# A two-layer trunk on one core: weights of the start in halves, attention norms spread over the head loop, Pool's remainders in pieces

## The chip, the cores and the metric

The kernel runs on one core of a Trainium2 chip. Five engines of that core run side by side, each with its own queue of instructions: TensorE (PE, matrix products), VectorE (DVE), ScalarE (ACT), GpSimd (Pool) and SyncE (SP, which issues nearly all transfers). The metric is the device time of one execution in microseconds (us); lower is better.

## What is computed

`x` is 256 tokens of 1024 numbers, all in fp32. Two layers are run, each a feed-forward part, a token mixer and another feed-forward part; the mixer of layer 0 is a state-space scan (Mamba-2), that of layer 1 an attention with low-rank queries and keys. The change touches the first feed-forward part and the attention:

```python
def rms_norm(x, w):
    return x * rsqrt(mean(x * x, -1) + 1e-6) * w

def swiglu(h, w_gate, w_up, w_down):              # 1024 -> 2816 -> 1024
    return (silu(h @ w_gate) * (h @ w_up)) @ w_down

def mla_mixer(h, positions, ...):                 # 16 heads
    proj = h @ w_in                               # 1024 -> 384 + 256 + 32
    cq = rms_norm(proj[..., :384], q_a_norm)
    ckv = rms_norm(proj[..., 384:640], kv_a_norm)
    k_rope = proj[..., 640:]
    q = (cq @ w_q_b).reshape(b, s, 16, 64 + 32)
    kv = (ckv @ w_kv_b).reshape(b, s, 16, 64 + 64)
    q_nope, q_rope = q[..., :64], q[..., 64:]
    k_nope, v = kv[..., :64], kv[..., 64:]
    # each of q_nope, q_rope, k_nope, k_rope: rms_norm over its own last axis
    # q_rope and k_rope are then turned by the position's angles
    o = causal_block_attention(q_nope, q_rope, k_nope, k_rope, v)   # softmax in blocks of 128 queries
    return o.reshape(b, s, 1024) @ w_out

for i in range(2):
    x = x + 0.5 * swiglu(rms_norm(x), ...)
    x = x + mixer_i(rms_norm(x))
    x = x + 0.5 * swiglu(rms_norm(x), ...)
```

## The kernel before

**Layout.** Features lie on the 128 partitions and the 256 tokens on the free axis, so `x` is eight slices of 128x256. The parts run one after the other: `ffn` 0, `ssm` 1, `ffn` 2, `ffn` 3, `mla` 4, `ffn` 5. The norm's factor for a token is applied after the products: the parts multiply `x` scaled by the norm's weight alone, and the token factors `rs` come in where the products are read.

**Weights.** All weights come as one stream in the order of use, in units of up to eight 128x128 tiles (512 KB). SP's queue loads a unit into one of AHEAD = 4 `raw` buffers. fp32 accuracy is reached by splitting: ACT rounds the unit (L119, `whi`), then `raw - whi` gives the remainder `wlo` (L121) on DVE, or on Pool for the units listed in POOL_UNITS. The rings of `whi` and `wlo` have SPLIT = 5 buffers. A tile is then two or three passes on PE (`mm2` L214, `mm3` L203 to L205, `mm3t` in `mla`). Two units of the attention (EARLY) are loaded and split during `ffn(3)`, in buffers of their own.

**Start.** SP issues `nw`, then slices of `x` and units of weights in turn, then the constants `sm` and `cst`. The first two units hold four tiles. Each slice of `x` is scaled and split (`xp`: ACT L232, DVE L233) and squared and summed on Pool (L239 to L243). After the first 32 tiles of `ffn(0)`, `make_rs` sums the squares on PE (L249), takes mean and epsilon on DVE (`rsv`, L253) and the power -1/2 on Pool (`rsc`, L257), and spreads the result on PE (L264); only then can the four open accumulators be read by the gated products (L320, L321) and given back.

**Attention.** `latent` writes cq and ckv in two parts. DVE turns the 32 rotary features of the keys into `kr`. `half(i)` then does eight heads: two groups of four heads of queries (`qc`), keys (`kc`), values (`vt`), with sums of squares by DVE reductions (L863, L879), then `rsqrt` by eleven dependent DVE instructions (L807 to L821), then the scaling of `qc` on DVE and of `kc` on Pool (L896), then `rope` with two products on Pool, two on DVE (L833) and two sums on DVE (L838, L841). `half(0)` and `half(1)` both run before the head loop. The loop over heads `h` turns heads h+2, h+3 (`to_heads`, L909, transposes on PE), makes the scores of head h (L947 to L952, with two mask products, `idb` times `neg`; then `mx` and `pr` on DVE and ACT, L957 to L966), turns the weights of head h-2 (`turned`, L974, and the copy `pT`), multiplies the values of head h-4 (L987, L988), and from h = 12 on does one step of the output projection. In `values` two heads share one accumulator, one on each half of the array's columns.

**Order.** The Tile scheduler places the instructions of each engine from the program's order and its own estimates; each engine then works through its list in that order, and waits where an input is missing.

Of the kernel before, what the change touches and what calls it, by code (L numbers as in the profile page):

```python
# [10 lines left out]
F32 = mybir.dt.float32  # L11
# [36 lines left out]
def unit_sizes():  # L48
# [13 lines left out]


POOL_UNITS = [MLA0 + n for n in (15, *range(17, 26))]
EARLY = (MLA0 + 10, MLA0 + 16)


class Stream:
# [11 lines left out]

    def load(self, upto):
        while self.loaded < min(upto, len(self.sizes)):
            u = self.loaded
            if u in EARLY:
# [4 lines left out]
            self.nc.sync.dma_start(  # L89
                t[:, : n * P],  # L90
                self.src[self.offs[u] : self.offs[u + 1]].rearrange("(p c) -> p c", p=P),
            )
            self.raw[u] = t
            self.loaded += 1

    def cut(self, upto):
        while self.split < min(upto, len(self.sizes)):
# [8 lines left out]
            if self.sizes[u] == KD * NARROW // P:  # L106
# [12 lines left out]
            self.nc.scalar.copy(hi[:, :n], raw[:, :n])  # L119
            eng = self.nc.gpsimd if u in POOL_UNITS else self.nc.vector  # L120
            eng.tensor_tensor(  # L121
                out=lo[:, :n], in0=raw[:, :n], in1=hi[:, :n].bitcast(F32), op=ALU.subtract
            )
            self.parts[u] = (hi, lo)

    def early(self, pool, u):
# [6 lines left out]
        hi = pool.tile([P, n], F32R, name=f"hi{u}", bufs=1)  # L133
        lo = pool.tile([P, n], F32R, name=f"lo{u}", bufs=1)
# [6 lines left out]
    def ahead(self):  # L141
        self.load(self.unit + SPLIT)
        self.cut(self.unit + SPLIT - 1)
# [21 lines left out]
def trunk(ctx: ExitStack, tc: tile.TileContext, xt, pos, wts, small, consts, out):  # L165
# [19 lines left out]
    nc.sync.dma_start(nw, small[:, S_NW : S_NW + KD])  # L185
    ws = Stream(nc, wp, wts)
    for i, (d0, d1) in enumerate(((0, 1), (1, 2), (2, 4), (4, 6), (6, 8))):
        nc.sync.dma_start(x[:, d0:d1], xt[:, d0:d1])
        ws.load(i + 1)
    nc.sync.dma_start(sm, small)  # L190
    nc.sync.dma_start(cst, consts)
# [93 lines left out]
    def use_x(n, d):  # L285
# [5 lines left out]
        scaled_parts(xh[:, d], xl[:, d], x[:, d], w)  # L291
        if d == 0:
            accs[n] = sp.tile([P, T], F32, tag="xsq", name="xsq")
# [18 lines left out]
    def ffn(n, nxt, early=()):  # L312
        early = list(early)
        with tc.tile_pool(name="fp", bufs=2) as fp:
# [20 lines left out]
            for k in range(KD):  # L335
                for o in ps:
                    mm2(o, ws.next(), xp[:, k], k == 0, k == KD - 1)
            rs, rh = make_rs(n, True)
            for j in range(2):
                gated(j, ps[2 * j], ps[2 * j + 1])  # L340
            for q in range(2, KF):
# [5 lines left out]
                if early and q % 2 == 0:  # L347
# [389 lines left out]
    def mla(n, nxt):  # L737
        with tc.tile_pool(name="lp", bufs=2) as lp:
# [14 lines left out]
            neg = one("neg", [P, P], BF16)  # L753
            nc.vector.tensor_copy(idb, ident)
            nc.vector.tensor_copy(neg, cst[:, C_NEG : C_NEG + P])

            oh = one("oh", [P, 8, T], F32R)
            ol = one("ol", [P, 8, T], F32R)
# [23 lines left out]
            p0, p1 = acc_ps(), acc_ps()  # L782
            for k in range(KD):
                a = (xh[:, k], xl[:, k], k == 0, k == KD - 1)
                mm3(p0[:, :T], ws.next(), *a)
# [412 lines left out]
```

## Time and profile before

| | |
|---|---|
| median of three runs | 1120.55 us (1119.16 to 1121.17) |
| the profiled execution | 1121.53 us, of which the span of the trace is 1119.4 us |
| PE busy | 1083.5 us (97%) |
| DVE busy | 846.4 us (76%) |
| ACT busy | 642.2 us (57%) |
| Pool busy | 216.9 us (19%) |
| mean granted clock of PE | 0.989 |
| transfers | 191.58 MB, mean 171 GB/s |

"Busy" is the union of an engine's instructions, so an engine at 97% can still be the one that waits in the remaining 3%. The granted clock is the share of full speed at which PE was allowed to run: 1.00 is the upper of its two levels (2.4 GHz), 0.50 the lower (1.2 GHz).

### The profile page before, as it was taken

The numbers are of one execution on the slowest core, as the hardware profiler recorded it, in microseconds if no ns is written. First come the engines' busy times: TensorE is split into PE (matmuls) and PEld (weight loads), VectorE is DVE, ScalarE is ACT, GpSimd is POOL, SyncE is SP. The second block draws the span as 40 slices with busy tenths as digits, with TensorE's granted clock in tenths as the row PEclk, the third lists the DMA queues.
The fourth block names the chain that finished last, engine by engine and source line by source line (L and its number), as shares of the span: only waits on it lengthen the run. The fifth ranks groups of instructions, "written<-read, shape, count | busy, mean of one in ns | idle before, by whom it ended". The sixth has DMA issues, their size and how long they took to land.

```text
span 1119.4 us, 18325 instructions
## 1 busy us (share of the span) xinstructions
PE 1083.5 (97%) x6902; PEld 967.1 (86%) x6902; DVE 846.4 (76%) x1370; ACT 642.2 (57%) x1102; POOL 216.9 (19%) x201
## 2 busy tenths in 40 slices
PE   7999999998899998999999999999996999999998
PEld 6888888998899997888888888888995788888887
DVE  7877776789978767877776787767779768877663
ACT  6766544667775744655544565554565546655541
POOL 7000012203523236000012200002347035000000
PEclk9999999999999999999999999999998999999999
DMA  7766565555445444655555565555443025665661
GB/s 243 229 188 190 192 187 172 177 191 191 160 148 186 137 149 133 202 187 186 186 184 180 192 226 188 188 188 181 162 145 103 1 66 171 214 189 185 189 202 55
DMA packets 55320, 191.58 MB, mean 171 GB/s; under 512 B 6304, under 2 KB 8384, under 8 KB 55232
## 3 DMA queue, kind: packets, MB, share of 16 engines
q1 hardware_dynamic: 55200, 190.41, 52.2%
q8 instruction: 54, 0.88, 0.3%
q14 instruction: 34, 0.28, 0.1%
q0 software_dynamic: 32, 0.00, 0.0%
HBM read 189.31 MB, written 1.08 MB: 170 GB/s over the span
## 4 chain that ended last, share of the span: by engine, by line
PE 57%; DVE 4%; POOL 1%; ACT 1%; issue 0%; ACTq 0%; DVEq 0%
PE acc L214 31%; PE misc L214 16%; PE acc L203 2%; PE acc L204 2%; PE acc L205 2%; PE acc L987 1%; POOL xsq L243 1%; DVE qc L896 1%; POOL sq L242 1%; PE misc L949 1%; PE misc L909 1%; PE misc L974 0%; PE misc L947 0%; PE acc L988 0%; DVE ro L833 0%; ACT whi L119 0%
## 5 line engine op out<-in xcount | busy, mean ns | idle before, releaser
L121 DVE TENSOR_TENSOR wlo<-raw,whi 128x1024 fp32r<-128x1024 f32 (+3 forms) x345 | 433.6, 1259 | 153.6 <-ACT whi L119 152.5
L119 ACT CAST whi<-raw 128x1024 fp32r<-128x1024 f32 (+3 forms) x355 | 364.8, 1032 | 258.0 <-PE acc L214 137.5
L214 PE MATMUL misc<-xp,whi 128*128 128x512 f32 x704 | 278.0, 398 | 1.4 <-ACT whi L119 1.4
L214 PE MATMUL acc<-xp,whi 128*128 128x512 f32 x704 | 274.4, 393 | 0.0
L214 PE MATMUL acc<-ap,whi 128*128 128x512 f32 x616 | 215.5, 397 | 0.0
L214 PE MATMUL misc<-xp,wlo 128*128 128x256 f32 x704 | 196.5, 281 | 2.6 <-DVE wlo L121 2.5
L214 PE MATMUL acc<-xp,wlo 128*128 128x256 f32 x704 | 197.1, 282 | 0.5 <-DVE wlo L121 0.3
L214 PE MATMUL acc<-ap,wlo 128*128 128x256 f32 x616 | 167.7, 281 | 0.0
L214 PEld LDWEIGHTS acc<-xp,whi 128*128 128x128 f32 x704 | 131.9, 188 | 32.0
L214 PEld LDWEIGHTS misc<-xp,whi 128*128 128x128 f32 x704 | 132.0, 188 | 23.9 <-ACT whi L119 1.6
L214 PEld LDWEIGHTS misc<-xp,wlo 128*128 128x128 f32 x704 | 132.4, 188 | 11.0 <-DVE wlo L121 4.0
L214 PEld LDWEIGHTS acc<-ap,whi 128*128 128x128 f32 x616 | 113.9, 188 | 25.6
L214 PEld LDWEIGHTS acc<-xp,wlo 128*128 128x128 f32 x704 | 132.5, 188 | 1.8 <-DVE wlo L121 1.1
L214 PEld LDWEIGHTS acc<-ap,wlo 128*128 128x128 f32 x616 | 115.4, 188 | 2.8
L320 ACT COPY g<-misc 128x256 f32<-128x256 f32 x88 | 32.7, 371 | 79.6 <-PE misc L214 79.4
L204 PE MATMUL acc<-xp,whi 128*128 128x256 f32 x264 | 74.6, 283 | 0.0
L203 PE MATMUL acc<-xp,whi 128*128 128x256 f32 x264 | 74.4, 283 | 0.0
L239 POOL TENSOR_TENSOR xsq<-x 128x256 f32<-128x256 f32 x6 | 3.7, 614 | 364.6 <-DVE x L364 350.1
L205 PE MATMUL acc<-xp,wlo 128*128 128x256 f32 x264 | 74.2, 281 | 0.0
L242 POOL TENSOR_TENSOR sq<-x 128x256 f32<-128x256 f32 x42 | 40.3, 967 | 114.5 <-DVE x L364 112.1
L243 POOL TENSOR_TENSOR xsq<-xsq,sq 128x256 f32<-128x256 f32 x45 | 51.7, 1149 | 2.6
L321 DVE TENSOR_TENSOR g<-misc,g 128x256 f32<-128x256 f32 x88 | 37.1, 422 | 18.2 <-ACT g L320 18.2
(249 smaller groups left out, 1908.3 us busy)
## 6 DMA issues: line engine op xcount, KB each, us to landing
raw<-wts SPq DMA_DIRECT2D x341, 512.0 KB, 3.9
acb<-acd SPq DMA_DIRECT2D x8, 512.0 KB, 4.1
raw<-wts SPq DMA_DIRECT2D x8, 256.0 KB, 2.8
raw<-wts SPq DMA_DIRECT2D x4, 384.0 KB, 3.0
out<-x SPq DMA_DIRECT2D x8, 128.0 KB, 3.4
x<-xt SPq DMA_DIRECT2D x3, 256.0 KB, 6.3
raw<-wts SPq DMA_DIRECT2D x4, 192.0 KB, 2.3
sm<-small SPq DMA_DIRECT2D x1, 283.5 KB, 6.6
```

Source lines behind the costliest of these rows:

```text
L119: self.nc.scalar.copy(hi[:, :n], raw[:, :n])
L121: eng.tensor_tensor(out=lo[:, :n], in0=raw[:, :n], in1=hi[:, :n].bitcast(F32), op=ALU.subtract)
L203: nc.tensor.matmul(o, w[0], h, start=start, stop=False)
L204: nc.tensor.matmul(o, w[0], l, start=False, stop=False)
L205: nc.tensor.matmul(o, w[1], h, start=False, stop=stop)
L214: nc.tensor.matmul(dst, a, b, start=start and i == 0, stop=stop and i == 1)
L242: nc.gpsimd.tensor_tensor(out=sq, in0=src, in1=src, op=ALU.mult)
L243: nc.gpsimd.tensor_tensor(out=acc, in0=acc, in1=sq, op=ALU.add)
L320: nc.scalar.copy(t, ps[:, T:])
L321: nc.vector.tensor_tensor(out=t, in0=ps[:, :T], in1=t, op=ALU.add)
L896: eng.tensor_tensor(out=a, in0=a, in1=r[:, b, o].unsqueeze(2).broadcast_to(list(a.shape)), op=ALU.mult,)
L909: nc.tensor.transpose(ps[:QK, o : o + P], src[:, b, h0 + h], ident)
```

## The change

1. **Start.** The first four units all hold eight tiles, and are loaded, rounded and subtracted in halves of 512 columns; each half's load follows the load of one slice of `x`. `nw` is loaded by Pool's queue. `cst` and `sm` are loaded after the first 32 tiles' code. The squares of the first norm are made by two ACT instructions of 1024 columns and three DVE sums; Pool takes no part in them.
2. **EARLY** holds four units (all those of keys and values) in place of two.
3. **Attention norms.** Keys' and values' latents come first. The norms of the heads are three: `a` (keys of heads 0 to 7, queries of 0 to 3), `b` (queries 4 to 7), `c` (keys and queries 8 to 15). `a` and `b` run before the loop; the four steps of `c` are put into the head loop at h = 1 to 4, each behind the scores of head h-2. Pool does none of the scalings and rotary products; ACT copies the rotary keys into `kc`.
4. **Head loop.** Both masks are one product of 256 columns; the values of two heads are multiplied together at odd h.
5. **Pool.** POOL_UNITS are eight units of the output projection; each remainder is four pieces of 256 columns, and waits for the last scaling made so far by a norm.

```diff
-    ffn = [4] * 2 + cut(KF * KD * 2 - 8) + cut(KD * KF)
+    ffn = cut(KF * KD * 2) + cut(KD * KF)
-    mla = cut(KD * 5) + narrow + ([6, 3] * 2 + [8] * 2) * 2 + cut(64)
+    mla = cut(KD * 5) + narrow + ([8] + [6, 3] * 2 + [8]) * 2 + cut(64)
...
-POOL_UNITS = [MLA0 + n for n in (15, *range(17, 26))]
-EARLY = (MLA0 + 10, MLA0 + 16)
+HALVED = KD // 2
+POOL_UNITS = [MLA0 + n for n in range(18, 26)]
+EARLY = (MLA0 + 6, MLA0 + 11, MLA0 + 12, MLA0 + 17)
...
+            for c in self.pieces(u):
+                if u < HALVED:
+                    next(self.beside)
+                self.nc.sync.dma_start(t[:, c], src[:, c])
...
+            for c in self.pieces(u):
+                self.nc.scalar.copy(hi[:, c], raw[:, c])
+            for c in self.pieces(u, 4 if u in POOL_UNITS else 1):
+                ins = eng.tensor_tensor(
+                    out=lo[:, c], in0=raw[:, c], in1=hi[:, c].bitcast(F32), op=ALU.subtract
+                )
+                if u in POOL_UNITS and self.behind is not None:
+                    self.tc.add_manual_dep(
+                        ins.ins, self.behind.ins.name,
...
-    nc.sync.dma_start(nw, small[:, S_NW : S_NW + KD])
+    nc.gpsimd.dma_start(nw, small[:, S_NW : S_NW + KD])
...
+            if n == 0:
+                nc.sync.dma_start(cst, consts)
+                nc.sync.dma_start(sm, small)
+                sq = fp.tile([P, KD, T], F32, name="x2", bufs=1)
+                for h in (slice(0, 4), slice(4, 8)):
+                    nc.scalar.activation(sq[:, h], x[:, h], AF.Square)
+                for h in (4, 2, 1):
+                    nc.vector.tensor_tensor(
+                        out=sq[:, :h], in0=sq[:, :h], in1=sq[:, h : 2 * h], op=ALU.add
+                    )
+                accs[n] = sq[:, 0]
...
-            half(0)
-            half(1)
+            for b in range(NB):
+                nc.scalar.copy(kc[:, b, :, NOPE:], krt[:, b].broadcast_to([P, MH, ROPE]))
+            keys(0, ss[0])
+            queries(0, ss[0], 8, 4)
+            for _ in normed("a", ss[0], (0, 8), (0, 4)):
+                pass
+            queries(1, ss[1], 0, 4)
+            for _ in normed("b", ss[1], (4, 4), (4, 8)):
+                pass
+            values_of(0)
+            ws.limit = MLA0 + 18
+            steps = normed("c", ss[2], (8, 16), (8, 16))
+            def second(h):
+                if h == 0:
+                    keys(1, ss[2])
+                    queries(2, ss[2], 8, 8)
+                    queries(3, ss[2], 12, 8)
+                    values_of(1)
+                if 0 < h < 5:
+                    step = next(steps)
...
+                if h == 5:
+                    ws.limit = len(SIZES)
+                    ws.cut(MLA0 + 21)
...
-                if 0 <= h - 4 < MH:
-                    values(h - 4, pTs.pop(h - 4))
+                if 0 <= h - 4 < MH and h % 2:
+                    values((h - 5) // 2, [pTs.pop(h - 5), pTs.pop(h - 4)])
+                second(h)
```

ACT's first instructions, before (`whi` of 512 columns is a unit of four tiles):

```order
L183 COPY used<-ones 128x1
L232 ACTIVATE xp<-x,nw 128x256
L119 CAST whi<-raw 128x512
L232 ACTIVATE xp<-x,nw 128x256
L119 CAST whi<-raw 128x512
L232 ACTIVATE xp<-x,nw 128x256 x2
L119 CAST whi<-raw 128x1024
```

ACT's first instructions, after (`x_249` is the tile of squares):

```order
L204 COPY used<-ones 128x1
L131 CAST whi<-raw 128x512
L256 ACTIVATE xp<-x,nw 128x256 x2
L131 CAST whi<-raw 128x512
L256 ACTIVATE xp<-x,nw 128x256
L131 CAST whi<-raw 128x512
L256 ACTIVATE xp<-x,nw 128x256
L370 ACTIVATE x_249<-x 128x1024
L131 CAST whi<-raw 128x512
L256 ACTIVATE xp<-x,nw 128x256
```

The first rounding of weights moved ahead of the first slice of `x`, every rounding became one of 512 columns, and the squares entered ACT's list.

DVE at the end of the second half's sums of squares, before (all of it ahead of the first scores):

```order
L863 TENSOR_REDUCE ss_9200<-qsq 128x4 x3
L879 TENSOR_REDUCE ss_9200<-ksq 128x8
L863 TENSOR_REDUCE ss_9200<-qsq 128x4 x2
L889 TENSOR_SCALAR ss_9200<-ss_9200 128x2x8
L879 TENSOR_REDUCE ss_9200<-ksq 128x8
L838 TENSOR_TENSOR qc<-ro 128x2x8x16
L841 TENSOR_TENSOR qc<-ro 128x2x8x16
```

DVE in the first heads of the loop, after (`nyc` is the result of norm `c`'s `rsqrt`):

```order
L1050 TENSOR_SCALAR pr<-pr,sums 128x128
L1050 TENSOR_SCALAR pr<-pr,sums 128x256
L930 TENSOR_TENSOR kc<-kc,nyc 128x2x8x64
L1041 TENSOR_REDUCE mx<-misc 128x1
L1048 RECIPROCAL sums<-sums 128x2
L1061 COPY pT<-misc 128x384
L1041 TENSOR_REDUCE mx<-misc 128x1
L1050 TENSOR_SCALAR pr<-pr,sums 128x128
L1050 TENSOR_SCALAR pr<-pr,sums 128x256
L930 TENSOR_TENSOR qc<-qc,nyc 128x2x8x32
```

The scalings of the second half now stand between the scores of the first heads, not ahead of them.

PE in the head loop, before (`pT`, `vt` are the values' operands; L909 turns heads):

```order
L974 MATMUL misc<-cst,pr 128x128 x3
L909 MATMUL misc<-cst,kc 96x128 x4
L987 MATMUL acc<-pT,vt 64x256
L988 MATMUL acc<-pT,vt 64x128
L909 MATMUL misc<-cst,qc 96x128 x4
L947 MATMUL misc<-kT,qT 128x128
```

PE in the head loop, after:

```order
L1057 MATMUL misc<-cst,pr 128x128 x3
L963 MATMUL misc<-cst,kc 96x128 x4
L1072 MATMUL acc<-pT,vt 64x256
L963 MATMUL misc<-cst,qc 96x128 x4
L1072 MATMUL acc<-pT,vt 64x256
L1072 MATMUL acc<-pT,vt 64x128 x2
L1032 MATMUL misc<-kT,qT 128x256
```

The values of two heads moved together, with a turn of queries between the first product of 256 columns and the second, while the two of 128 columns stand side by side.

## Rows read from the trace of the kernel before

**Rows 1.** Waits of PE, 823 to 874 us: engine, line, releaser: total, times, longest.

```profile
PE misc L909 <- DVE qc L841: 9.7, 1, 9.7
```

**Rows 2.** Stretches: PE, PEld, DVE, ACT, POOL busy (count), PEclk, DMA share, GB/s.

```profile
823.98:873.69 49.71, 37.54 (x202) 32.05 (x201) 44.68 (x112) 32.67 (x63) 28.40 (x20) 0.90 0.37 113
826.00:845.00 19.00, 19.00 (x101) 17.53 (x101) 17.21 (x53) 16.09 (x28) 9.41 (x8) 1.00 0.52 158
845.00:860.00 15.00, 4.92 (x22) 3.29 (x22) 14.90 (x20) 7.71 (x12) 14.35 (x8) 0.81 0.40 129
873.00:895.00 22.00, 21.82 (x148) 16.38 (x147) 14.78 (x51) 11.91 (x42) 0.00 (x0) 1.00 0.00 1
```

**Rows 3.** Stretches around PE's long wait, same columns.

```profile
854.26:859.68 5.42, 0.00 (x0) 0.00 (x1) 5.42 (x5) 2.77 (x5) 5.08 (x3) 0.50 0.61 174
859.68:864.50 4.82, 4.82 (x21) 4.22 (x22) 2.49 (x13) 1.91 (x4) 2.04 (x2) 0.50 0.23 77
```

**Rows 4.** Stretches of the start, same columns.

```profile
6.43:27.02 20.59, 16.59 (x85) 12.77 (x86) 19.68 (x31) 14.03 (x23) 18.14 (x23) 1.00 0.77 272
9.00:11.00 2.00, 1.51 (x8) 1.06 (x8) 1.52 (x3) 1.65 (x3) 1.92 (x4) 1.00 1.04 417
```

**Rows 5.** PE at the start, order of time: start, us, instruction [idle before <-releaser].

```profile
6.43 0.50 PE L214 MATMUL misc<-xp,whi 128*128 128x512 f32 x1 [1.42 <-ACT whi L119]
...
21.48 0.50 PE L249 MATMUL misc<-ones,xsq 128*128 128x1 f32 x4
...
27.02 0.43 PE L264 MATMUL misc<-cst,rsc 128*128 128x128 f32 x2 [0.87 <-POOL rsc L257]
```

**Rows 6.** ACT, DVE and Pool at the start, same columns, one engine after another.

```profile
5.76 0.62 ACT L119 CAST whi<-raw 128x512 fp32r<-128x512 f32 x1 [1.52 <-DMA raw<-wts]
...
4.28 0.48 DVE L233 SCALAR_TENSOR_TENSOR xp<-x,nw,xp 128x256 fp32r<-128x256 f32 x1
...
8.11 0.68 DVE L121 TENSOR_TENSOR wlo<-raw,whi 128x512 fp32r<-128x512 f32 x1
...
25.33 1.64 POOL L257 TENSOR_TENSOR rsc<-rsv,mhalf 128x2 f32<-128x2 f32 x1 [0.23 <-DVE rsv L253]
```

**Rows 7.** Pool, then DVE, in the first norm of the heads, same columns.

```profile
837.80 5.24 POOL L121 TENSOR_TENSOR wlo<-raw,whi 128x1024 fp32r<-128x1024 f32 x2 [0.40 <-ACT whi L119]
...
838.34 2.41 DVE L821 SCALAR_TENSOR_TENSOR nyh<-nth,nyh 128x48 f32<-128x48 f32 x1
...
843.14 0.21 DVE L818 SCALAR_TENSOR_TENSOR nth<-nth,nvh 128x48 f32<-128x48 f32 x1
843.39 0.21 DVE L821 SCALAR_TENSOR_TENSOR nyh<-nth,nyh 128x48 f32<-128x48 f32 x1
```

**Rows 8.** DVE's groups, 824 to 873.69 us: instruction | busy, mean ns | idle before.

```profile
L879 DVE TENSOR_REDUCE ss<-ksq 128x8 f32<-128x512 f32 x4 | 2.7, 675 | 0.0
...
L121 DVE TENSOR_TENSOR wlo<-raw,whi 128x768 fp32r<-128x768 f32 x2 | 1.9, 958 | 0.0
```

**Rows 9.** DVE in the attention, order of time, columns as in rows 5.

```profile
823.98 0.41 DVE L799 TENSOR_TENSOR kr<-acc,rs 64x256 f32<-64x256 f32 x1
...
828.68 0.60 DVE L863 TENSOR_REDUCE ss<-qsq 128x4 f32<-128x256 f32 x2
...
871.59 0.41 DVE L838 TENSOR_TENSOR qc<-ro 128x256 f32<-128x256 f32 x1
```

**Rows 10.** PE in the head loop, and one row of the scan (`ssm`), same columns.

```profile
873.69 0.49 PE L974 MATMUL misc<-cst,pr 128*128 128x128 f32 x3
...
874.94 0.65 PE L987 MATMUL acc<-pT,vt 128*64 128x256 f32 x2
...
290.96 0.66 PE L571 MATMUL misc<-dec,xd 128*64 128x256 f32 x4
```

**Rows 11.** Pool and DVE late in the head loop, same columns.

```profile
908.24 2.38 POOL L121 TENSOR_TENSOR wlo<-raw,whi 128x1024 fp32r<-128x1024 f32 x1 [8.04 <-ACT whi L119]
...
908.86 2.10 DVE L966 TENSOR_SCALAR pr<-pr,sums 128x128 f32<-128x128 f32 x2
```

More of the change, by code (lines that the diff above doesn't have):

```diff
@@ L79, in __init__ @@
         self.unit, self.pos = 0, 0
+        self.tc, self.behind = None, None
+        self.limit = len(SIZES)
     def load(self, upto):
@@ L118, in cut @@
             lo = self.pool.tile([P, UNIT * P], F32R, tag="wlo", name="wlo", bufs=SPLIT)
-            self.nc.scalar.copy(hi[:, :n], raw[:, :n])
             eng = self.nc.gpsimd if u in POOL_UNITS else self.nc.vector
-            eng.tensor_tensor(
-                out=lo[:, :n], in0=raw[:, :n], in1=hi[:, :n].bitcast(F32), op=ALU.subtract
-            )
+            for c in self.pieces(u):
[7 more added lines that the diff above has]
+                        ins.ins, self.behind.ins.name,
+                        mybir.DependencyInfo(
+                            mybir.DependencyClass.Sync, mybir.DependencyReason.DATA
+                        ),
+                        reason="the port that DVE and Pool share",
+                    )
             self.parts[u] = (hi, lo)
@@ L184, in trunk, with load_x @@
     nw = cp.tile([P, KD], F32, name="nw")
-    nc.sync.dma_start(nw, small[:, S_NW : S_NW + KD])
+    nc.gpsimd.dma_start(nw, small[:, S_NW : S_NW + KD])
+    def load_x():
+        for d in range(KD):
+            yield nc.sync.dma_start(x[:, d], xt[:, d])
     ws = Stream(nc, wp, wts)
[L187 to L191, printed above, removed]
+    ws.tc = tc
+    ws.beside = load_x()
+    ws.load(HALVED)
     ident = cst[:, C_ID : C_ID + P]
@@ L346, in ffn @@
                 gated(q, pg, pu)
-                if early and q % 2 == 0:
+                if early and q % 4 == 0:
                     ws.early(*early.pop(0))
@@ new lines, in normed, with scaled @@
+            def normed(name, ss, hk, hq):
+                (k0, k1), (q0, q1) = hk, hq
+                nk, nq = k1 - k0, q1 - q0
+                ro = ss[:, :, nk + nq :]
+                first = nc.vector.tensor_scalar_mul(ro, ro, NOPE / ROPE)
+                r = rsqrt(ss.rearrange("p b s -> p (b s)"), NOPE, name)
+                r = r.rearrange("p (b s) -> p b s", b=NB)
+                yield first
+                def scaled(s0, a):
+                    return nc.vector.tensor_tensor(
+                        out=a, in0=a,
+                        in1=r[:, :, s0 : s0 + a.shape[2]].unsqueeze(3)
+                        .broadcast_to(list(a.shape)),
+                        op=ALU.mult,
+                    )
+                if nk:
+                    yield scaled(0, kc[:, :, k0:k1, :NOPE])
+                a = qc[:, :, q0:q1, NOPE:]
+                first = scaled(nk + nq, a)
+                rope(a, a, nq, qtab)
+                yield first
+                ws.behind = scaled(nk, qc[:, :, q0:q1, :NOPE])
+                yield ws.behind
@@ L880, in half, with values_of @@
+            def values_of(i):
                 w = [ws.next(4), ws.next(4)]
@@ L955, in scores @@
                 pr = lp.tile([P, 3 * P], F32, tag="pr", name="pr", bufs=4)
-                for b, sl in ((0, slice(0, P)), (1, slice(P, 3 * P))):
+                for b, sl in ((0, slice(T, 3 * P)), (1, slice(0, T))):
                     nc.vector.tensor_reduce(
```

197 lines of the change are left out of this document (99 added, 98 removed).

## The prediction

> **What bounds the kernel now.** I read the busy shares first: TensorE is busy nearly throughout, so only a place where it stands idle, or runs at its lower clock, can give time back. Its list of waits names one large place: 9.7 us in the attention, where the first turn of heads waits for DVE's last rotary sum (`qc`, L841) [rows 1]. The stretches around it show the pattern [rows 2]: from 826 to 845 PE is busy for all of its 19 us, from 845 to 860 for 4.9 of 15, while DVE is busy for 14.9 and Pool for 14.35 of those 15; from 873 on PE is full again. After the wait PE works at half its clock: 4.82 us of work at a granted clock of 0.50, the lower of its two levels, which is 2.4 us lost, after 5.42 us in which it ran nothing [rows 3]. The second place is the start: between its first weight product (6.43) and the spread of the first norm (27.02) PE works 16.59 of 20.59 us, and the last wait there is on Pool's power [rows 4, 5]. The feed-forward parts elsewhere are PE's own work, and the change leaves their products as they are; the two further units fetched early in `ffn(3)` add a load, an ACT rounding and a Pool remainder each, to a stage where PE waits for none of these engines, so I cost them at nothing (bounds: 0 to one remainder on Pool, 2.4 us [rows 11], if PE ever waited for one).
>
> **The sum's base** is the profiled execution, 1121.53 us. It lies 1.0 above the median of the runs, which I take off at the end.
>
> **Part 1, the start.** What goes: the whole-unit steps of load, rounding and remainder, and Pool's chain of squares. What comes: a rounding of 512 columns at 0.62 and a remainder at 0.68 per half [rows 6].
> - First product: its weights land at 5.76 before [rows 6]; one issue less stands ahead of them on SP (`nw` moved to Pool's queue; the two units' start-to-start issues are some 0.45 apart, an estimate), so 5.3. The rounding (0.62), the remainder of weights (0.68) and the low part of `x` (0.48) follow; in the new order the first rounding is ahead of the first slices of `x`, so 5.3 + 0.62 + 0.68 + 0.48 = 7.1, against 6.43: 0.67 later. `nw` from Pool's queue can be late by as much without cost, since ACT first waits for the weights.
> - From there PE's work to the spread of the norm is the same 16.59 us [rows 4]. If it never waited, the spread would come at 7.1 + 16.6 = 23.7 instead of 27.02: -3.3. That is one bound. What could eat it up is the supply of halves. PE makes eight products of a half, at 16.59 us for 85 some 0.195 each [rows 4], so 1.5 us per half. A half and its slice of `x` are 384 KB, 0.94 us at the 417 GB/s of 9 to 11 us, where the transfers are full (DMA share 1.04 [rows 4]); DVE needs 0.68 + 0.48 = 1.16 us per half [rows 6], ACT about as much and the squarings besides. So each of the three keeps ahead of PE, but ACT with little to spare. The other bound is 0, if PE waits behind the squarings as long as it now waits for whole units.
> - The norm itself: two squarings of 1024 columns on ACT and sums of 1024, 512 and 256 on DVE are done well before the 32nd tile's column sums; then sums, `rsv` and the same power on Pool (1.64 [rows 6]) run beside PE's next group, as before, without the squares ahead of them. `cst` and `sm`, issued behind two more units, are first read at the spread; they displace no weights any more.
> I take -2.8, inside 0 to -3.3, nearer to PE's own pace, since all three suppliers are faster than PE.
>
> **Part 2, the norms of the heads.** Removed: Pool's share (two rotary products, the keys' scaling), the wait of DVE behind Pool, and the second half's norm from ahead of the loop. Before, from `kr` at 823.98 [rows 9] to the turn of head 2's weights at 873.69 [rows 10] pass 49.7 us; PE works 37.5 of them, 2.4 of which are lost to the clock [rows 2, 3]. The same work of PE has to be done by the same point after, so PE alone would allow 35.1 us: -14.6. I think DVE comes later than that. Its list up to that point, at undisturbed prices:
> - remainders of four query units, 2 x 0.96 and 2 x 0.55 (the smaller by columns) [rows 8]: 3.0
> - sums of squares, 4 x 0.68 [rows 8] and 8 pairs x 0.60 [rows 9]: 7.5
> - four `rsqrt` chains of 11 dependent instructions, 0.21 each and 0.23 to 0.25 from start to start [rows 7]: 10.3
> - the rotary key's preparation, a dozen instructions of about 0.21 [rows 7]: 2.6
> - scalings: two of 1024 columns, the rest 256 or 512 columns, at 0.41 per 256 [rows 9] falling to 1.2 per 1024 by the remainders' rate [rows 8]: 5.0
> - rotary products and sums, two sets of six at some 0.22 and one set of six at 0.35 to 0.41 [rows 9]: 4.7
> - scores of three heads and the maximum of the fourth: DVE is busy 14.78 us for 51 instructions in the loop, 6.5 per head, so 1.9 us per head [rows 2]: 6.4
> The sum is 39.5 us, so the third turn at 863.5 instead of 873.69: **-10.2**. The prices of before can't be taken, since there DVE stood behind Pool: one instruction of 48 columns took 2.41 us beside Pool's remainder, its like 0.21 a little later [rows 7]. Bounds: -14.6 if PE sets the end; -6 if the chain is a tenth longer and a half-clock spell stays.
>
> **Part 3, the rest of the loop and Pool's pieces.** The loop before is PE's: 21.82 of 22 us [rows 2], about 2.8 us a head against DVE's 1.9.
> - Values: in the scan four products on the two column halves take 0.66 us together; in the loop two take 0.65 [rows 10]. So two heads' products can overlap. In the new order only those of 128 columns stand together; between those of 256 a turn of queries stands. A pair of 128 columns is a third of a pair's values, an estimated 0.2 us saved for each of eight pairs: -1.6 (bounds: 0; all overlapped, 8 x 0.8 = -6.4, by 0.65 and a half of it for the shorter ones, less what they already share).
> - Masks: one product in place of two, -0.4. At the third turn one more head's values are already done: -0.8.
> - Norm `c` leaves a rotary set and two scalings, some 3.4 us on DVE, for heads 3 and 4; DVE then needs more than PE per head: +1.0.
> - Pool's pieces: beside a remainder of 1024 columns that took 2.38 us, two instructions of 128 columns on DVE took 2.10 us, where 256 columns alone take 0.41 [rows 9, 11]. A quarter of it lasts 0.6. DVE has 0.9 us a head to spare. Of 32 pieces, 12 come close together behind h = 5; bounds 0 to +3.6 (12 x 0.6 over four heads, less 4 x 0.9). I take +0.7, since most pieces meet a DVE that has room.
> Sum: -1.1. The Trainium skill (SBUF — State Buffer, "SBUF: two separate sides") says that DVE and GpSimd share one port pair as an exclusive lock, held for a whole instruction, the loser blocked. Row 908.86 agrees; by that rule every piece could hold up DVE for its length, and this term would be the bound +3.6 instead of +0.7.
>
> **Sum:** 1121.5 - 2.8 - 10.2 - 1.1 = 1107.4; less 1.0 for the median: **1106.4**.
>
> **Rivals.**
> - *PE sets the end of the norms* (start -3.3, norms -14.6, loop -1.1, median -1.0): 1101.5; with all values overlapping too, 4.8 lower, 1096.7. For it: 35.1 us of PE work in that stretch. Against it: DVE's list is longer than that, and hardly anything on it can go. The Trainium skill (TensorEngine Tiling (Array Packing), "Key Properties") says that different tiles of the array execute in parallel; the scan's row agrees, but the order of the loop parts the longer products.
> - *The gains are halved:* the start gains nothing (0), DVE's chain ends at -6, pieces cost +3.6 (loop +1.8): 1121.5 - 6 + 1.8 - 1.0 = 1116.3. For it: DVE in this stretch is dependent small instructions, with ACT's exponentials between; against it: the scheduler interleaves two chains.
> - *Slower, by the clock:* with the one long wait replaced by many short ones between 830 and 873, PE may run at its lower level. 35.1 us of work at half the clock are 70; it decides from the point where PE works over 15 us of them at half: 35.1 + 15 is as long as before, and with all of it the end is 20 later, 1138. For it: the row at 0.50 after a wait [rows 3]. Against it: with PE busy, though in pieces, the clock held 1.00 from 826 to 845 [rows 2].
> - *It doesn't do what it says:* norm `b`, still ahead of the loop, keeps the first turn of heads waiting as before; DVE's list up to there is some 12 us shorter, so I hold it unlikely. Time: 1120.
>
> **Chances:** forecast (1103 to 1110) 0.62, PE-bound 0.12, halved gains 0.16, slower 0.06, no effect 0.04. The range 1100 to 1114 leaves out the lower part of the second, the upper part of the third and the last two. About 0.2% is what a measurement can tell from no change; faster by more than that 0.90, within it 0.04, slower 0.06.
>
> **What would show it.** The wait of the first turn of heads should shrink from 9.7 us to under 4, and the stretch at 0.50 with it; DVE should be busy without a break from `kr` to the third turn, some 39 us; the spread of the first norm should come at about 24 us. In the loop DVE's instructions beside Pool's pieces should be longer by 0.6 us at most. I am wrong if `rsqrt` instructions still take over a microsecond each, if PE's waits only move to scores and `pT`, or if the granted clock stays at 0.50 in the loop.

## The result and the profile after

The changed kernel takes 1104.37 us (median of four runs, 1102.76 to 1106.05), the kernel before 1120.74 on the same chip: a ratio of 0.9857, 95% interval 0.9839 to 0.9874, so 16 us faster, where 14 were forecast. The profiled execution is one of 1104.49 us with a span of 1102.7, against 1121.53 and 1119.4: 17 us. Its busy shares, engine by engine:

```profile
PE 1079.8 (98%) x6886; PEld 964.3 (87%) x6886; DVE 838.8 (76%) x1396; ACT 643.1 (58%) x1105; POOL 195.7 (18%) x201
```

Five marks cut both executions into the same stretches. They are, in order of time in the trace of the changed kernel, the spread of the first norm, the first column sum of the scan (`ssm`), `kr`, the turn of head 2's weights, and the first column sum of the last feed-forward part (start, us, instruction; between the brackets the idle time before it and what ended it):

```profile
23.09 0.43 PE L288 MATMUL misc<-cst,rsc 128*128 128x128 f32 x2 [1.14 <-POOL rsc L281]
...
200.26 0.28 PE L273 MATMUL misc<-ones,xsq 128*128 128x1 f32 x2
...
819.32 0.42 DVE L837 TENSOR_TENSOR kr<-acc,rs 64x256 f32<-64x256 f32 x1
...
856.85 0.52 PE L1057 MATMUL misc<-cst,pr 128*128 128x128 f32 x3 [0.88 <-ACT pr L1044]
...
923.04 0.50 PE L273 MATMUL misc<-ones,xsq 128*128 128x1 f32 x4
```

In the kernel before the first, third and fourth are in [rows 5, 9, 10], and the other two are:

```profile
202.64 0.28 PE L249 MATMUL misc<-ones,xsq 128*128 128x1 f32 x2
...
940.10 0.50 PE L249 MATMUL misc<-ones,xsq 128*128 128x1 f32 x4
```

(The profile puts the four column sums of a mark in one row or in two; the start of the first counts.) Out of these:

| stretch | before | after | difference | forecast |
|---|---|---|---|---|
| to the spread of the first norm | 27.02 | 23.09 | -3.9 | -2.8 |
| to the scan | 175.6 | 177.2 | +1.6 | 0 |
| scan, two feed-forward parts, latents, to `kr` | 621.3 | 619.1 | -2.3 | 0 |
| `kr` to the third turn | 49.7 | 37.5 | -12.2 | -10.2 |
| third turn to the end of the attention | 66.4 | 66.2 | -0.2 | -1.1 |
| last feed-forward part | 179.3 | 179.7 | +0.4 | 0 |

The largest change is where it was looked for. The stretches of the changed kernel, to be held against [rows 2] (busy time of PE, PEld, DVE, ACT, Pool, then the granted clock): from `kr` to the third turn as a whole, 19 us within it, and the stretch in which Pool runs 20 of its pieces.

```profile
819.32:856.85 37.53, 34.72 (x197) 30.04 (x196) 32.69 (x133) 30.77 (x65) 1.77 (x3) 1.00 0.20 63
826.00:845.00 19.00, 19.00 (x106) 17.36 (x105) 17.82 (x82) 18.58 (x34) 0.00 (x0) 1.00 0.27 85
858.53:872.47 13.94, 12.68 (x72) 8.84 (x72) 11.68 (x30) 8.89 (x27) 13.94 (x20) 0.88 0.46 145
```

PE works 34.7 of 37.5 us at full clock, where it worked 37.5 of 49.7. Pool, busy for 28.4 us of that stretch before, is busy for 1.8. In place of one wait of 9.7 us PE has these from `kr` on, of which 2.8 us lie ahead of the third turn and 1.6 behind it (engine, line, releaser: total, times, longest):

```profile
PE misc L1057 <- ACT pr L1044: 1.2, 2, 0.9
PE misc L963 <- DVE pT L1061: 1.0, 1, 1.0
PE misc L1057 <- DVE sums L1048: 0.6, 1, 0.6
PE misc L1032 <- ACT kT L968: 0.6, 1, 0.6
PE misc L963 <- ACT pr L1044: 0.5, 1, 0.5
PE acc L1072 <- DVE pT L1061: 0.5, 1, 0.5
```

### The profile page after: what moved, and what is told of

It is laid out like the page before. It is cut to its first block, busy times and chain, and to the rows that moved or that the text cites. A ratio compares the mean times of both kernels' runs of the same rounds, so it can differ in the third digit from the quotient of the medians.

```text
span 1102.7 us, 18308 instructions
## 1 busy us (share of the span) xinstructions
PE 1079.8 (98%) x6886; PEld 964.3 (87%) x6886; DVE 838.8 (76%) x1396; ACT 643.1 (58%) x1105; POOL 195.7 (18%) x201
## 4 chain that ended last, share of the span: by engine, by line
PE 61%; DVE 2%; ACT 0%; issue 0%; ACTq 0%; DVEq 0%
PE acc L238 32%; PE misc L238 17%; PE acc L227 2%; PE acc L228 2%; PE acc L229 2%; PE acc L1072 1%; PE acc L248 1%; PE acc L247 1%; PE acc L249 1%; PE misc L963 1%; PE misc L1032 1%; PE misc L1057 0%; DVE pr L1050 0%; DVE mx L1041 0%; PE misc L1033 0%; PE misc L273 0%
## 5 line engine op out<-in xcount | busy, mean ns | idle before, releaser
L134 DVE TENSOR_TENSOR wlo<-raw,whi 128x1024 fp32r<-128x1024 f32 (+2 forms) x345 | 429.4, 1247 | 155.0 <-ACT whi L131 153.8
L131 ACT CAST whi<-raw 128x1024 fp32r<-128x1024 f32 (+2 forms) x353 | 362.8, 1032 | 252.5 <-PE acc L238 132.9
L238 PEld LDWEIGHTS acc<-xp,whi 128*128 128x128 f32 x704 | 131.9, 188 | 32.2
L346 ACT COPY g<-misc 128x256 f32<-128x256 f32 x88 | 32.7, 371 | 77.1 <-PE misc L238 77.1
L266 POOL TENSOR_TENSOR sq<-x 128x256 f32<-128x256 f32 x35 | 31.7, 912 | 111.2 <-DVE x L402 111.2
L227 PEld LDWEIGHTS acc<-xp,whi 128*128 128x128 f32 x264 | 49.7, 189 | 0.3 <-issue 0.3
```

The costliest lines, as they stand in the source:

```text
L131: self.nc.scalar.copy(hi[:, c], raw[:, c])
L134: ins = eng.tensor_tensor(out=lo[:, c], in0=raw[:, c], in1=hi[:, c].bitcast(F32), op=ALU.subtract)
L227: nc.tensor.matmul(o, w[0], h, start=start, stop=False)
L238: nc.tensor.matmul(dst, a, b, start=start and i == 0, stop=stop and i == 1)
L266: nc.gpsimd.tensor_tensor(out=sq, in0=src, in1=src, op=ALU.mult)
L346: nc.scalar.copy(t, ps[:, T:])
```

## The experiments

Each kernel is the changed one with one thing altered, unless it says otherwise, and each was compared with the kernel before on the same chip. "kr to third" and "third to end" are the stretches of the table above, from each profile.

| kernel | median us | ratio to before (95%) | kr to third | third to end |
|---|---|---|---|---|
| before | 1120.74 | 1 | 49.7 | 66.4 |
| changed | 1104.37 | 0.9857 (0.9839 to 0.9874) | 37.5 | 66.2 |
| old_start | 1108.69 | 0.9897 (0.9884 to 0.9911) | 37.6 | 66.2 |
| start_only (on before) | 1117.08 | 0.9972 (0.9959 to 0.9985) | 50.6 | 66.4 |
| c_ahead | 1107.47 | 0.9884 (0.9870 to 0.9897) | 41.7 | 64.4 |
| pool_norms | 1104.91 | 0.9863 (0.9849 to 0.9876) | 39.3 | 65.6 |
| pool_whole | 1107.59 | 0.9869 (0.9852 to 0.9885) | 37.5 | 68.7 |
| whole_free | 1110.32 | 0.9895 (0.9875 to 0.9915) | 46.7 | 63.3 |
| no_pool_units | 1108.12 | 0.9873 (0.9856 to 0.9890) | 37.6 | 68.6 |
| early_two | 1105.09 | 0.9853 (0.9830 to 0.9877) | 39.1 | 65.5 |
| all_three | 1114.44 | 0.9943 (0.9927 to 0.9960) | 50.9 | 62.4 |
| warm_spread | 1105.06 | 0.9864 (0.9849 to 0.9880) | 37.6 | 64.5 |
| later_steps | 1103.16 | 0.9841 (0.9828 to 0.9854) | 36.0 | 67.1 |
| best | 1103.64 | 0.9854 (0.9827 to 0.9880) | 36.0 | 66.6 |

Medians of different rows come from different chips (before: 1120.0 to 1122.1), so the ratios are to be compared. An interval is some 1.5 to 3 us wide either way; single stretches of a profile tell smaller things apart: `kr` to the third turn is 37.5 or 37.6 us in the changed kernel and in the four that don't alter it there (`old_start`, `pool_whole`, `no_pool_units`, `warm_spread`). Not always, though: `start_only` has the code of before there and 50.6 us instead of 49.7, with 3.4 us more at the lower clock.

### The start, undone and alone

`old_start` has the start of before in the changed kernel, `start_only` the new start in the kernel before:

```diff
-HALVED = KD // 2
+HALVED = 0
-    ffn = cut(KF * KD * 2) + cut(KD * KF)
+    ffn = [4] * 2 + cut(KF * KD * 2 - 8) + cut(KD * KF)
...
+    for i, (d0, d1) in enumerate(((0, 1), (1, 2), (2, 4), (4, 6), (6, 8))):
+        nc.sync.dma_start(x[:, d0:d1], xt[:, d0:d1])
+        ws.load(i + 1)
```

> The changed kernel with the start of before (two units of four tiles, whole units, squares on Pool, nw on SP). The trace of the changed kernel gained 3.93 us up to the spread of the first norm, but only 2.38 us of it are left at the end of the first feed-forward part, where its products come every 0.1761 us instead of 0.1737. Theory: that slower pace belongs to the new start, so undoing the start costs only 2.4 us, and the pace is 0.174 again: 1106.8 us, with 1.5 us either way for half-clock spells in the scan. Rival: the pace has nothing to do with the start; undoing it costs 3.9 us, 1108.3, and the pace stays 0.176.

> The kernel before with the new start alone (four units in halves beside the slices of x, squares on ACT and DVE, nw on Pool's queue). Theory that the parts add up: spread of the first norm near 23.1 instead of 27.0, pace 0.176 in the first feed-forward part, so 2.4 us faster than before, 1118.3. Rival that the start's gain reaches the end whole: 1116.8. Rival that a later stage gives it back: 1120.5.

Undoing the start costs 0.40% (0.9897 against 0.9857), 4.5 us; alone it brings 0.28%, 3.1 us. The totals lie nearer to the rivals, but their intervals also take in the 2.4 us of the theories; it is the pace that decides. The slower pace in the first feed-forward part, which hid 1.6 us of the gain in the profile of the changed kernel, is no part of the start: `start_only` and `c_ahead` have the new start and the quicker pace. (In `old_start`, where the rival expected the slower one, it is quick too.) Counted over the same 90 us (50 to 140, PE busy throughout), the kernel before, the changed kernel and `c_ahead`, in that order:

```profile
50.00:140.00 90.00, 90.00 (x520) 79.02 (x519) 68.17 (x113) 54.34 (x98) 0.00 (x0) 1.00 0.61 190
...
50.00:140.00 90.00, 90.00 (x513) 78.38 (x512) 66.75 (x110) 52.94 (x95) 0.00 (x0) 1.00 0.61 187
...
50.00:140.00 90.00, 90.00 (x520) 79.05 (x519) 67.87 (x110) 53.04 (x95) 0.00 (x0) 1.00 0.58 192
```

513 products in the profiled execution of the changed kernel, 520 in `c_ahead`, at the same granted clock of 1.00; of the 14 profiles eleven have the quicker pace, three (the changed kernel, `pool_whole`, `warm_spread`) the slower, and most of the 14 have the same code in this stretch. What sets the pace was not found.

The start itself also varies between executions. With the same code the spread of the first norm comes between 22.61 and 23.84 in eleven kernels with the new start (all but `best`, which alters it), and at 27.02 and 28.26 in the two with the old one; in the second of these 3.4 us at the lower clock, from 13.33 on, lie ahead of it.

### Norm c ahead of the loop, and Pool in the norms

```diff
                     values_of(1)
+                    for _ in steps:
+                        pass
-                if 0 < h < 5:
-                    step = next(steps)
```

> The changed kernel with norm c (keys and queries of heads 8 to 15) ahead of the first scores instead of in the head loop. Theory: spreading it is what keeps TensorE fed, since the maxima of heads 0 and 1 then stand behind a chain of 2.6 us and 5.3 us of scalings and rotary products: TensorE idle 6 to 8 us more before the first turn of weights, and half clock after it: 1111 to 1114 us. Rival: up to the third turn of weights DVE does nearly the same work in either order, so only the steps that now come later cost, 3.4 us: 1107.8.

It costs 0.27%, 3 us, and `kr` to the third turn grows by 4.1 while the rest shrinks by 1.8: the rival's bookkeeping. Up to the third turn PE waits 4.9 us instead of 2.8, not 6 to 8 more; the half clock that the theory expected did come, in one spell of 6.8 us. `pool_norms` gives Pool its small products back:

```diff
-                    nc.vector.tensor_tensor(
+                    eng = nc.gpsimd if j < 2 else nc.vector
+                    eng.tensor_tensor(
                         out=t, in0=part, in1=tab.unsqueeze(2).broadcast_to([P, NB, nh, 16]),
...
-                yield scaled(0, kc[:, :, k0:k1, :NOPE])
+                yield scaled(0, kc[:, :, k0:k1, :NOPE], nc.gpsimd)
```

> The changed kernel with Pool back in the norms: two of the four rotary products and the scaling of the keys on Pool, as before; all else unchanged, the norms still spread. Theory that the shared work with Pool was the cost: DVE's last rotary sum waits for Pool in each of the three norms (before, two products of 256 columns took Pool over a microsecond each): 3 to 6 us slower than the changed kernel, 1107.5 to 1110.5. Rival: moving Pool's large remainders out of this stage was what counted, and Pool's small products run beside DVE's other work: within 1 us of 1104.4.

It is within 1 us (0.9863 against 0.9857). So "without Pool" in the norms is not what made the gain, as long as nothing else of Pool's stands there. The 1.8 us between `kr` and the third turn are mostly clock: PE waits 3.2 us there instead of 2.8, but 3.4 us of its work run at 0.50.

### Pool's remainders: whole, whole and free, none

`pool_whole` makes one instruction of each remainder; `whole_free` also takes away the wait for the norm and the limit on cutting ahead; `no_pool_units` gives them to DVE.

```diff
-            for c in self.pieces(u, 4 if u in POOL_UNITS else 1):
+            for c in self.pieces(u):
...
-                if u in POOL_UNITS and self.behind is not None:
-                    self.tc.add_manual_dep(
...
-            ws.limit = MLA0 + 18
...
-POOL_UNITS = [MLA0 + n for n in range(18, 26)]
+POOL_UNITS = []
```

> The changed kernel with each of Pool's eight remainders as one instruction of 1024 columns instead of four of 256; they still wait for the norm's last scaling. In the trace of the changed kernel 20 pieces run without a break from 858.5 to 872.5, and DVE's pairs of weight scalings, 0.55 us alone, take 1.02 to 1.61 beside them. Theory: a DVE instruction stands for what is left of Pool's instruction, so with whole ones it stands up to 2.4 us, and TensorE, which has 0.9 us a head to spare, waits: 1105.5 to 1108. Rival: longer but fewer stands, the same in sum: 1104.4 within 1 us.

> The changed kernel with whole remainders on Pool that wait for nothing but their weights (no wait for the norm's last scaling, no limit on how far ahead units are cut), so Pool's first four or five run while the norms do, as in the kernel before. Theory: it is this meeting of Pool's large remainders with the norms' chains that made DVE late before; up to five times 2.4 us of it: 1109 to 1115, with rsqrt instructions of over a microsecond in the trace. Rival: TensorE sets the pace there until the last projection, and DVE has 4 us idle in it: under 2 us slower, below 1106.5.

> The changed kernel with all eight remainders of the output projection on DVE, none on Pool in the attention. Theory that Pool's pieces are worth their cost: DVE has 8 x 1.23 = 9.8 us more, half of it in the stretch from 847 to 858 where TensorE already waits for DVE, against some 3 us of stands that go: 1106.5 to 1110. Rival that the shared port costs as much as the work: 1103.5 to 1105.5.

`whole_free` costs 4.3 us in all and 9.2 of the 12.2 us between `kr` and the third turn. Its trace shows how, first Pool, then DVE in norm `b`'s chain, then PE's first waits:

```profile
838.96 10.23 POOL L134 TENSOR_TENSOR wlo<-raw,whi 128x1024 fp32r<-128x1024 f32 x4 [6.10 <-ACT whi L131]
...
839.82 2.39 DVE L847 TENSOR_TENSOR ntb<-nyb 128x16 f32<-128x16 f32 x1
842.14 0.60 DVE L906 TENSOR_REDUCE ss<-qsq 128x4 f32<-128x256 f32 x2
842.66 1.97 DVE L867 TENSOR_TENSOR qc<-ro 128x128 f32<-128x128 f32 x1
844.56 2.42 DVE L870 TENSOR_TENSOR qc<-ro 128x128 f32<-128x128 f32 x1
846.91 2.32 DVE L848 SCALAR_TENSOR_TENSOR ntb<-ntb,nvb 128x16 f32<-128x16 f32 x1
849.26 0.17 DVE L851 SCALAR_TENSOR_TENSOR nyb<-ntb,nyb 128x16 f32<-128x16 f32 x1
...
PE misc L955 <- DVE qc L870: 4.7, 1, 4.7
PE misc L1020 <- ACT kT L960: 2.1, 1, 2.1
```

Four remainders of some 2.6 us each on Pool, and four small instructions of DVE that last nearly as long each, one per remainder; the two reductions between them, with one input, run on. When Pool is done, the next instruction of the same chain takes 0.17. PE's wait of 4.7 us ends at 847.04, and the lower clock begins within it. The stretch from `kr` to the third turn and the longer of its two spells:

```profile
818.85:865.58 46.73, 38.56 (x197) 32.68 (x196) 42.95 (x133) 32.20 (x66) 14.43 (x8) 0.89 0.34 106
...
845.38:852.21 6.83, 5.17 (x19) 4.33 (x20) 6.73 (x15) 2.26 (x5) 3.81 (x2) 0.50 0.73 218
```

So the 9.2 us are two things: PE stands idle for 8.2 us instead of 2.8, which is 5.4, and is busy for 38.6 us instead of 34.7 with the same products, since 8.4 us of its work run at 0.50. The theory holds, at its lower end; the total is less than the 9.2 us, since behind the third turn 2.9 us come back (63.3 instead of 66.2), where those remainders no longer run.

`pool_whole` costs 0.12% by its ratio, which the intervals don't part from none, but 2.6 us in the stretch behind the third turn, with one wait of PE on `pT` that the changed kernel has not, and a pair of scalings (0.55 us alone) of 3.52:

```profile
860.48 3.52 DVE L1050 TENSOR_SCALAR pr<-pr,sums 128x128 f32<-128x128 f32 x2
...
PE misc L1032 <- DVE pT L1061: 2.6, 1, 2.6
```

So the wholeness of the remainders alone costs nothing ahead of the third turn (37.5); in `whole_free` it is their place that counts. `no_pool_units` costs 2.4 us behind the third turn and 0.16% (1.8 us) by its ratio, at the edge of what was expected and within the intervals: by the profile Pool's share is worth having, the total doesn't show it.

### Two units early instead of four

```diff
-EARLY = (MLA0 + 6, MLA0 + 11, MLA0 + 12, MLA0 + 17)
+EARLY = (MLA0 + 6, MLA0 + 12)
```

> The changed kernel with two units fetched and split early (the keys' weights of both halves) instead of four; the values' two units come in the stream, with 2 x 1.23 us more on DVE, 2 x 1.04 on ACT and 1 MB more to load in the attention. Theory: DVE is idle for 4 us in pieces before the loop, so it is hidden: within 1 us of 1104.4. Rival: DVE is the bound of this stretch, as the prediction had it, and the 2.5 us come out whole: 1106.9.

0.9853 against 0.9857: no difference. The stretch to the third turn is 1.6 us longer, the rest 0.6 shorter, and no spell of the lower clock follows.

### All three undone

`all_three` joins `whole_free`, `pool_norms` and `c_ahead`.

> The changed kernel with three things undone at once: Pool's remainders whole and free to run in the norms, two rotary products and the keys' scaling on Pool, norm c ahead of the loop. From kr to the third turn of weights the kernel before took 49.7 us, the changed one 37.5, with the remainders alone undone 46.7, with norm c alone 41.7, with Pool in the norms alone 39.3. Theory: what the change gained there is Pool and DVE standing in each other's way, and the three make it worse for each other: 49 to 55 us, attention about as long as before, 1115 to 1119. Rival: much of the gain comes from what is not undone here (order of keys, queries and values, pairs of values, one mask): the attention stays 5 us or more shorter than before, 1110 to 1113.

`kr` to the third turn is 50.9 us, no shorter than before (49.7): the theory's mechanism. The total, 1114.44, lies between the theory's range and the rival's, and so does the attention, 2.9 us shorter than before. PE's waits there are three, of 4.7, 4.0 and 2.1 us, and DVE's pair of scalings of queries takes 3.53:

```profile
857.88 2.41 POOL L923 TENSOR_TENSOR kc<-kc,nyc 128x1024 f32<-128x1024 f32 x1 [3.29 <-DVE nyc L851]
...
857.83 3.53 DVE L923 TENSOR_TENSOR qc<-qc,nyc 128x512 f32<-128x512 f32 x2
```

Undoing these three thus takes back all of the 12 us; undone alone they cost 9.2, 4.1 and 1.8 there. Here too the lower clock takes its share: 17.1 us of the stretch are at 0.50, 10.2 in the kernel before, none in the changed one. The new order of keys, queries and values, which all kernels but before and `start_only` have, was not tried alone; in this run, without the other three, nothing of the gain is left there. The rest of the attention is 4 us shorter than before (62.4 against 66.4), with pairs of values, one mask and five remainders done ahead of it; these were not parted.

### Three attempts at more

`warm_spread` runs one power on Pool at the start and cuts Pool's units one by one; `later_steps` moves two steps of norm `c`; `best` has both orders of the loop, and DVE's mean (`rsv`) ahead of two sums:

```diff
-                if 0 < h < 5:
+                if h in (1, 2, 4, 5):
...
-                if h == 5:
-                    ws.limit = len(SIZES)
-                    ws.cut(MLA0 + 21)
+                if h in (5, 7, 9, 11):
+                    if h > 5:
+                        ws.behind = done[h - 2]
+                    ws.cut(MLA0 + 19 + (h - 5) // 2)
...
+    nc.gpsimd.tensor_tensor(out=warm, in0=warm, in1=mhalf[:, :NB], op=ALU.pow)
```

> The changed kernel with two additions: one power of two columns on Pool at the very start, and Pool's units cut one by one at h = 5, 7, 9, 11, each behind the scores of head h-2, not three at once behind the norm. Theory: Pool's first power takes 1.58 us because it is the first of its kind (later ones take 0.70), and TensorE waits 1.14 us for it, so the wait shrinks to 0.3 or less; and spread pieces meet a DVE that has room, so TensorE's 1.6 us of waits behind the third turn fall below 1: together about 1.5 us faster than the changed kernel, 1103. Rival: the first power is long for another reason and the pieces block DVE as often as before: 1104.4.

> The changed kernel with the four steps of norm c at h = 1, 2, 4 and 5 instead of 1 to 4. Theory: from the first scores to the third turn TensorE waits 2.8 us in five places for DVE and ACT, because rotary products and scalings stand between the scores of heads 1 and 2; two of the four later take about 1 us off: 1103.4. Rival: the same work only waits elsewhere, behind the third turn, where Pool's pieces then start later too: 1104.4 or up to 1 us more.

> The changed kernel with three orders altered: norm c's steps at h = 1, 2, 4, 5; Pool's units cut at h = 5, 7, 9, 11; and the mean of the first norm on DVE ahead of two sums of products that read PSUM, so that Pool's power no longer runs beside a remainder. Theory: the power took 1.58 us because DVE's remainder of 1.21 us started 0.24 us ahead of it and held the shared port; now it takes 0.70 and TensorE's wait of 1.14 us falls below 0.3; kr to the third turn 36.0, kr to the end of the attention 101 to 102 instead of 103.7: 2.5 to 3.5 us faster than the changed kernel, 1101 to 1102. Rival: the power is as long as before and the two orders of the loop don't add: 1103.2 or more.

The theory of the first power falls: in `warm_spread` the added power takes 0.73 us, the norm's own again 1.62, and PE waits 1.13 for it. What stands beside it is DVE. In the changed kernel, Pool's power and the remainder that DVE starts just ahead of it; then the same two in `best`, where DVE does two sums that read PSUM first:

```profile
21.46 1.58 POOL L281 TENSOR_TENSOR rsc<-rsv,mhalf 128x2 f32<-128x2 f32 x1 [18.85 <-DVE rsv L277]
...
21.22 1.21 DVE L134 TENSOR_TENSOR wlo<-raw,whi 128x1024 fp32r<-128x1024 f32 x1
...
20.69 0.72 POOL L283 TENSOR_TENSOR rsc<-rsv,mhalf 128x2 f32<-128x2 f32 x1 [18.09 <-DVE rsv L279]
...
20.79 0.41 DVE L349 TENSOR_TENSOR u<-acc,u 128x256 f32<-128x256 f32 x1
21.12 1.22 DVE L134 TENSOR_TENSOR wlo<-raw,whi 128x1024 fp32r<-128x1024 f32 x1
```

The power of 1.58 us ends 0.61 after the remainder does (22.43), and takes 0.72 without it: the port is held against Pool as it is held against DVE. Being the first is not the reason: in the same trace a power at 404.43, begun 0.06 us behind a remainder, takes 1.73, and one at 303.04, with no DVE instruction beside it, 0.70. In `best` the spread of the norm comes at 21.66, without a wait. Of the loop's two orders the later steps do what they should to the third turn (36.0), but the two don't add behind it (66.6, more than `warm_spread`'s 64.5). By the total none of `best` (0.9854), `later_steps` (0.9841) and `warm_spread` (0.9864) can be told from the changed kernel (0.9857): the 2.5 to 3.5 us expected of `best` and the 1.5 of `warm_spread` did not come.

## Why the prediction was right, point by point

**The forecast** (1106.4, faster) holds, 2.0 us above the measured 1104.37. That it came so near is in part luck: in part 2 two terms were off by 6.8 and 4.8 us in opposite directions.

**Part 1, the start: mis-sized, on three terms.** The first product came at 6.06, not 7.1: the landing of the first half, put at 5.3, was 4.09, and the steps behind it took 1.97 us where 1.78 were worked out. (The 5.76 from which the 5.3 came was a late one: `old_start`, with the same order of loads as before, has 4.61.) PE's work from there to the spread is the last row: 15.59 us for 85 products, where 16.59 was taken over for as many; why they ran closer together is not shown.

```profile
4.09 0.62 ACT L131 CAST whi<-raw 128x512 fp32r<-128x512 f32 x1 [1.87 <-DMA raw<-wts]
...
6.06 0.50 PE L238 MATMUL misc<-xp,whi 128*128 128x512 f32 x1 [0.54 <-DVE xp L257]
...
6.06:23.09 17.03, 15.59 (x85) 12.83 (x86) 15.34 (x31) 13.57 (x23) 1.58 (x1) 1.00 0.93 333
```

The halves kept ahead of PE but for 0.2 us, as worked out. The bound of -3.3 was too small by 0.6, since it carried the late first product and the larger work. What was not in the sum is that the power on Pool, taken over at 1.64 [rows 6] and said to run beside PE's next group, outlasts that group by 1.1 us. The gain of the start reaches the end: 4.5 us undone, 3.1 alone.

**Part 2, the norms: right mechanism, -12.2 instead of -10.2.** The term that was mis-sized is DVE's list, 39.5 us. In the changed kernel DVE is busy for 32.7 of the 37.5 us, and idle for 4.8. So the list was 6.8 us too long, and the gaps, put at nothing, took back most of it. The four `rsqrt` chains, put at 10.3 us, took some 6.1, counted from each start to the next: instructions of two chains that alternate start 0.11 to 0.12 us apart, and only norm `c`'s last ones, alone, at 0.24. In the first of these rows two chains alternate, in the last two one runs alone:

```profile
833.53 0.19 DVE L856 SCALAR_TENSOR_TENSOR nta<-nta,nva 128x32 f32<-128x32 f32 x1
833.64 0.17 DVE L855 TENSOR_TENSOR ntb<-nyb 128x16 f32<-128x16 f32 x1
833.76 0.19 DVE L859 SCALAR_TENSOR_TENSOR nya<-nta,nya 128x32 f32<-128x32 f32 x1
...
848.24 0.20 DVE L855 TENSOR_TENSOR ntc<-nyc 128x48 f32<-128x48 f32 x1
848.48 0.21 DVE L856 SCALAR_TENSOR_TENSOR ntc<-ntc,nvc 128x48 f32<-128x48 f32 x1
```

So DVE was not "busy without a break", and the measured 37.5 us lie between the forecast's 39.5 and the rival "PE sets the end of the norms": its 35.1 us of PE work are there as 34.7, to which PE waits 2.8 us for DVE and ACT in the first scores. The first turn of heads, which waited 9.7 us, waits for nothing, and the lower clock after it is gone up to the third turn. The clock is the smaller share of the 12.2 us: PE idles 9.4 us less (2.8 instead of 12.2) and is busy 2.8 us less, of which 2.4 are the half clock of before [rows 3]. The prediction did not weigh the edits of this part against each other; the experiments do: keeping Pool's large remainders out of the norms is most of it.

**Part 3, the loop: right in sign, smaller.** -0.2 instead of -1.1. The term that is missing from the sum is the clock. From the third turn to the end of the attention before and after, and one spell of the lower clock that falls into the loop of the changed kernel:

```profile
873.69:940.10 66.41, 66.23 (x458) 55.53 (x457) 49.34 (x115) 34.39 (x87) 23.18 (x18) 1.00 0.22 71
...
856.85:923.04 66.19, 64.56 (x442) 53.34 (x442) 52.30 (x116) 34.89 (x84) 37.93 (x47) 0.97 0.36 109
...
859.40:862.80 3.40, 3.32 (x11) 2.12 (x12) 2.70 (x10) 1.99 (x8) 3.40 (x6) 0.50 0.08 13
```

PE's 3.3 us of work in that spell, at 0.50, cost 1.7. Without them its work is 62.9 us, 3.3 less than before, where values, masks and the head already done were put at -2.8 together. Against that stand 1.6 us of waits, where norm `c` and the pieces were put at +1.7. So these terms were near in sum, and the spell is what made the gain small; `warm_spread`, without one, has 64.5 us where the changed kernel has 66.2. The spell follows PE's waits of 0.9 and 1.0 us for `pr` and `pT` (the second ends at 859.48), while DVE works on norm `c`; the pieces, from 858.53 on, lengthen no DVE instruction before that. They do later: beside the 20 pieces, at 0.70 us each, DVE's pairs of scalings took 1.02 to 1.61 instead of 0.55, 3.1 us more in four pairs, of which these are the first and the last (Pool's row first):

```profile
858.53 13.94 POOL L134 TENSOR_TENSOR wlo<-raw,whi 128x256 fp32r<-128x256 f32 x20 [33.59 <-PE misc L1057]
...
859.79 1.02 DVE L1050 TENSOR_SCALAR pr<-pr,sums 128x128 f32<-128x128 f32 x2
...
871.01 1.61 DVE L1050 TENSOR_SCALAR pr<-pr,sums 128x128 f32<-128x128 f32 x2
```

The sentence from the Trainium skill (SBUF — State Buffer, "SBUF: two separate sides") is borne out by `whole_free` and by Pool's power, in both directions; that it would make the pieces cost their full bound of 3.6 us is not: of DVE's 3.1 us PE waited for 0.6, behind the last of these pairs, near the 0.7 that was taken.

**Outside the sum.** Between the scan's start and `kr` 2.3 us went that no edit there accounts for; PE is idle for 11.5 us there instead of 13.5, and why is open. The amount of lower clock is not it, since both profiles have 13.7 us of it up to `kr`; the 14 profiles have between 10.2 and 17.1, in spells whose places and lengths change. This and the slower pace (+1.6) nearly cancel, which is luck. The two further early units, put at nothing, show no cost in a profile: `ffn(3)` takes 180.6 us before and after.

**The rival by the clock** did not come: one spell of 3.4 us at the lower clock from `kr` to the end of the attention, against 10.2 us before.

## What to carry to other kernels

Where two engines share a port, look for small dependent instructions that last as long as the other engine's large one, and move the large ones out of that stretch or behind it; cutting them up limits what one meeting costs (at most 1.6 us for a pair of scalings here, 3.5 with whole remainders). When a wait of PE is priced, look at the granted clock behind it as well: in `whole_free` more than a third of the loss was half clock, not waiting. Price a list of dependent small instructions at its alone rate only where nothing else can be put between them. Measure such a change by the distance between two marks inside the profile as well as by the total, which moves by some 2 us on its own, and look whether a spell of the lower clock lies between the marks.

## What the runs showed of the hardware

- Pool's power of two columns takes 0.70 us, and 1.58 where DVE has just started a subtraction of two operands in SBUF (1.21 us); with sums that read PSUM beside it, 0.72.
- DVE instructions of 16 to 128 columns with two inputs took 1.97 to 2.42 us beside Pool's subtractions of 1024 columns (0.17 to 0.28 us for the same ones in the changed kernel, where Pool is idle there); the two reductions between them, with one input, were not held up (0.60 for both).
- PE ran 520 or 513 of the same products in 90 us in different executions, at a granted clock of 1.00 in both; the cause stays open.
- DVE instructions of 48 columns started 0.24 us apart in one dependent chain; those of 16 and 32 columns 0.11 to 0.12 apart where two chains alternated.
